# Two hybrid diffusion layers: the gate tiles of the first layer stand at other places in a hand-written order

## The chip, the cores and the metric

The kernel runs on one core of a Trainium2 chip. Its time is the device time of one launch in microseconds; three runs before the change took 2389.72, 2399.01 and 2402.41 us, so the median is 2399.01 us. Times inside a profile are counted from the start of its span.

## The reference, cut to what matters

Two layers work on 512 latent tokens and 256 context tokens of width 1024, in fp32. The part of a layer that this case is about:

```python
proj = a_lat @ w_in[l]             # and proj_c = a_ctx @ w_in[l] in the first layer
q, k, v  = proj[..., Q0:K0], proj[..., K0:V0], proj[..., V0:P0]
p = pool_branch(proj[..., P0:H0], ...)
y = hyena_branch(proj[..., H0:G0], ...)
a = diff_attn_branch(attn_o, ...)
g = sigmoid(proj[..., G0:].reshape(b, l, 3, D_MODEL))
merged = g[:, :, 0] * a + g[:, :, 1] * p + g[:, :, 2] * y
h = h + mod * (merged @ w_out)

def hyena_branch(u, ...):          # 3 x 512 channels
    u = short_conv(u, w_short, b_short)          # 3 taps along the tokens
    v, x1, x2 = split(u, 3)
    z = x1 * fft_long_conv(v, kf[:, 0], bias[0])
    y = x2 * fft_long_conv(z, kf[:, 1], bias[1])
    return y @ w_o
```

The gates `g` (3072 columns, 24 tiles of 128) depend on the normalised input alone and are needed only when the branches are merged, after the attention.

## The kernel before, in words

Activations lie with channels on the partitions and the 768 tokens in the free dimension. Every dense product is made by `units`: one tile of 128 output channels loads its weights (512 KB, a DMA on SP, three buffers `wr`), splits them into a high part (`wh`, ScalarE, line 252) and a low part (`wl`, VectorE, line 253), two buffers of each, and multiplies in three passes per 128 input channels, each for 512 latent and 256 context tokens (line 285). The result stands in an accumulator `d` of PSUM; in the first layer there are two of them. The tile's `evict` takes it out.

The first layer's stage of the long convolution runs over four groups of 128 channels, each with a latent and a context sequence. Its order is written out in the string `PROG[0]`, which `stage` reads letter by letter; capitals are the latent sequence, small letters the context:

- `F`, `f`: the filters and their spectra `K` (`filter_steps`: small matmuls, the window `dec`, absolute sums `fa`, transforms `gre` and `gim`, VectorE combinations at line 654); the latent `K` has one buffer
- `S`, `s`: transposes of the inputs (`vt`, `x1t`) and the forward transform `ur` (lines 767 to 769)
- `1`, `q`: the first spectral product on VectorE (`spectral`: lines 791, 794, 795)
- `M`, `m`: the way back to tokens (`zo`, line 863), the product with `x1`, and forward again
- `2`, `w`: the second spectral product
- `Z`, `z`: the last way back (`yo`, line 880) and the product with `x2` (line 881)
- `h`: one of the three row tiles that the next group needs (`v`, `x1`, `x2`). Its eviction `short` is a ScalarE activation (line 895) and four taps on VectorE (line 899)
- `g`: one gate tile. Its eviction `gate` is a sigmoid on ScalarE (line 935) and a store to device memory (line 936)

The letters give the order in which instructions are handed to a planner. It puts each engine's instructions into a fixed queue by its own costs: of those that are ready it takes the one handed in first. So a `g` or `h` runs while the steps ahead of it wait, and the first letters behind a step are those that fill beside it. Splits of weights are moved ahead (`ahead`, lines 252 and 253).

After group 3's `m` the left half of the fast memory is reopened for the attention. The tiles of head 0 follow (`fill`): value (`vtok`, line 1025), key and query (`roped`: a shuffle and products on VectorE, lines 999 to 1016). Then come the last two letters of the string (`w`, `z`), the right half is reopened, and the attention runs head by head, with `pool` tiles (buffers `pu`, line 1145) and the next head's tiles between. The row maxima of a head's scores are lines 1056 and 1059.

Of the kernel before, what the change touches and what calls it, by code (L numbers as in the profile page):

```python
# [36 lines left out]
NCOL = 129  # L37
FFN_PARTS = ((6, 5, 5, 6), (8, 7, 7))

PROG = ('FggS1ggMfs2gggZgqmFwhhhSz1gMfs2ggZqmFwhhhSz1ggMfs2ggggZggqmFwhhhSz1gMfs2gggZgqm wz',  # L40
        'FgS1gggMFhhhS2ggZgg1gMFhhhS2ggZgg1ggMFhhh2ggSZg1ggggM 2gZ')
HEAD = ("01rfrA23fcrVfBrfU", "01rfrfrA23fVcfBrfU")

# [101 lines left out]
def build(ctx: ExitStack, tc: tile.TileContext, io: dict, out: bass.AP, dbg=None):  # L145
# [763 lines left out]
    def layer(l, a, hs, first, prepare):  # L909
# [73 lines left out]

        early, late = PROG[l].split()
        for what in early:
# [540 lines left out]
```

## Time and profile before

| what | us |
|---|---|
| median of three runs | 2399.01 |
| lowest and highest of them | 2389.72, 2402.41 |
| profiled execution, its own time | 2393.87 |
| its span | 2392.1 |
| TensorE matmul busy, in the span | 2325.6 |
| TensorE weight loads busy | 1981.7 |
| VectorE busy | 1722.3 |
| ScalarE busy | 983.6 |

The busy time of an engine counts the time in which at least one of its instructions runs. Matmuls are pipelined, so that one starts before the one ahead of it has ended. An engine's queue runs in its order: an instruction that waits holds up those behind it. The stage of the long convolution lies between 70 and 500 us of the span; attention of the first layer follows.

### The profile page before, as it was taken

How to read it: one execution, taken by the hardware profiler on the slowest of the kernel's cores; microseconds unless marked ns; L12 is line 12 of the kernel's file. 1: busy time of each engine (PE TensorE's matmuls, PEld its weight loads, DVE VectorE, ACT ScalarE, POOL GpSimd, SP SyncE). 2: the span in 40 equal slices, each digit the busy share in tenths (PEclk: the TensorE clock that was granted, in tenths of full speed). 3: DMA queues.
4: the chain of work that ended last, by engine and by line, in shares of the span. 5: the costliest groups of instructions: out<-in, count | busy, mean ns of one | idle time of the engine just before them, and what ended most of it. 6: DMA issues, size and time to landing. Idle time of an engine off the chain costs nothing. (4 is left out here: it accounts for less than half of the span.)

```text
span 2392.1 us, 33306 instructions
## 1 busy us (share of the span) xinstructions
PE 2325.6 (97%) x12834; PEld 1981.7 (83%) x12834; DVE 1722.3 (72%) x3135; ACT 983.6 (41%) x1657; POOL 2.7 (0%) x8
## 2 busy tenths in 40 slices
PE   6999899999999999999999999999999999999998
PEld 3888688888878878888888888888888789888888
DVE  5688877999888785666768726899888778333336
ACT  6433334367762352121133424433377635312223
POOL 0000000000000000000000000000000000000000
PEclk9999899999989999999999999999999999999999
DMA  7222132321137543444725525344311444332324
GB/s 265 71 96 81 44 103 71 124 95 67 45 133 253 185 156 130 130 146 158 232 88 170 167 98 162 125 165 162 119 56 46 168 152 154 113 97 95 96 92 150
DMA packets 117801, 302.47 MB, mean 126 GB/s; under 512 B 13445, under 2 KB 27397, under 8 KB 116618
## 3 DMA queue, kind: packets, MB, share of 16 engines
q1 hardware_dynamic: 117642, 300.34, 37.9%
q8 instruction: 101, 1.65, 0.3%
q14 instruction: 58, 0.48, 0.1%
HBM read 266.74 MB, written 33.55 MB: 126 GB/s over the span
## 5 line engine op out<-in xcount | busy, mean ns | idle before, releaser
L252 ACT CAST wh<-wr 128x1024 fp32r<-128x1024 f32 (+3 forms) x327 | 331.0, 1013 | 933.2 <-PE d L285 756.1
L285 PE MATMUL d<-ah,wh 128*128 128x512 f32 (+1 forms) x2320 | 707.4, 354 | 6.8 <-ACT si L1371 2.8
L285 PE MATMUL d<-al,wh 128*128 128x512 f32 (+1 forms) x2320 | 709.9, 354 | 0.1
L285 PE MATMUL d<-ah,wl 128*128 128x512 f32 (+1 forms) x2320 | 706.6, 353 | 2.1 <-DVE wl L253 2.0
L253 DVE TENSOR_TENSOR wl<-wr,wh 128x1024 fp32r<-128x1024 f32 (+3 forms) x327 | 383.5, 1173 | 163.4 <-ACT wh L252 153.5
L285 PEld LDWEIGHTS d<-ah,wh 128*128 128x128 f32 x2320 | 387.8, 188 | 71.7 <-ACT si L1371 3.2
L285 PEld LDWEIGHTS d<-ah,wl 128*128 128x128 f32 x2320 | 388.8, 188 | 64.1 <-DVE wl L253 3.0
L285 PEld LDWEIGHTS d<-al,wh 128*128 128x128 f32 x2320 | 389.0, 188 | 61.5 <-DVE al L350 0.8
L489 DVE SCALAR_TENSOR_TENSOR junk<-mr,cb 128x512 bf16<-128x512 f32 x256 | 176.4, 689 | 13.4 <-DMA mr<-in_w_mod_rows_dram 8.2
L285 PE MATMUL d<-hh,wh 128*128 128x512 f32 (+1 forms) x584 | 179.1, 341 | 3.4 <-DVE h L1406 3.4
L285 PE MATMUL d<-hh,wl 128*128 128x512 f32 (+1 forms) x584 | 178.9, 341 | 0.0
L285 PE MATMUL d<-hl,wh 128*128 128x512 f32 (+1 forms) x584 | 178.7, 341 | 0.0
L1380 DVE TENSOR_TENSOR si<-d,si 128x512 f32<-128x512 f32 (+2 forms) x48 | 36.9, 768 | 174.3 <-PE d L285 174.3
L285 PE MATMUL d<-xs,wh 128*128 128x512 f32 x576 | 145.0, 358 | 0.8 <-ACT mx L1183 0.6
L1406 DVE SCALAR_TENSOR_TENSOR h<-d,mod,h 128x512 f32<-128x512 f32 (+1 forms) x96 | 58.5, 615 | 83.3 <-PE d L285 83.0
L285 PEld LDWEIGHTS d<-hh,wh 128*128 128x128 f32 x584 | 102.4, 190 | 17.9 <-issue 3.8
L285 PEld LDWEIGHTS d<-hl,wh 128*128 128x128 f32 x584 | 102.2, 190 | 13.6
L285 PEld LDWEIGHTS d<-hh,wl 128*128 128x128 f32 x584 | 102.4, 190 | 13.1
L285 PEld LDWEIGHTS d<-xs,wh 128*128 128x128 f32 x576 | 94.7, 189 | 18.1 <-ACT mx L1183 0.9
L285 PE MATMUL d<-xs,wl 128*128 128x512 f32 (+1 forms) x288 | 87.7, 358 | 0.0
L795 DVE TENSOR_TENSOR Y<-Y,T 128x1024 f32<-128x1024 f32 (+1 forms) x80 | 84.7, 1059 | 0.2
L794 DVE TENSOR_TENSOR T<-U,K 128x1024 f32<-128x1024 f32 (+1 forms) x80 | 83.1, 1059 | 0.0
(294 smaller groups left out, 3207.8 us busy)
## 6 DMA issues: line engine op xcount, KB each, us to landing
wr<-in_w_in_dram SPq DMA_DIRECT2D x104, 512.0 KB, 3.4
wr<-in_w_ffn_in_dram SPq DMA_DIRECT2D x96, 512.0 KB, 3.3
mr<-in_w_mod_rows_dram SPq DMA_DIRECT2D x160, 256.0 KB, 3.6
wr<-in_w_out_dram SPq DMA_DIRECT2D x32, 512.0 KB, 3.3
ksp<-K SPq DMA_DIRECT2D x28, 384.0 KB, 2.8
K<-ksp SPq DMA_DIRECT2D x8, 1344.0 KB, 7.7
wr<-in_w_ffn_out_dram SPq DMA_DIRECT2D x24, 448.0 KB, 3.4
gsp<-gt SPq DMA_DIRECT2D x24, 384.0 KB, 2.5
```

Source lines behind the costliest of these rows:

```text
L252: A.copy(hi, src)
L253: V.tensor_tensor(out=lo, in0=src, in1=hi.bitcast(F32), op=ALU.subtract)
L285: PE.matmul(o, w[:, c0:c0 + P], x[k][xi][:, c:c + nn], start=(k == 0 and pi == 0), stop=(k == K - 1 and pi == 2))
L489: V.scalar_tensor_tensor(out=junk[:], in0=raw[hf], scalar=1.0, in1=cb[v][hf][:, 0:512], op0=ALU.mult, op1=ALU.mult, accum_out=pv[:, v, hf, ...
L794: V.tensor_tensor(out=t[:], in0=ub, in1=kb, op=ALU.mult)
L795: V.tensor_tensor(out=y[:], in0=y[:], in1=t[:], op=ALU.add)
L1380: V.tensor_tensor(out=sg[f][:, cs], in0=o, in1=sg[f][:, cs], op=ALU.mult)
L1406: V.scalar_tensor_tensor(out=hs[d][:, cs], in0=o, scalar=mods[l][:, 40 + d, s:s + 1], in1=hs[d][:, cs], op0=ALU.mult, op1=ALU.add)
```

## The change

Only the string of the first layer changes. In group 0 one of the two gates between `F` and `S` is taken out; in group 1 a second gate is set beside the first product, a third beside the second product and one ahead of `q`; in group 2 the four gates beside the second product become three and the two ahead of `q` become one. The gates per group go from 8, 3, 8, 5 to 7, 6, 6, 5. The order of the gates among themselves, all other letters and the second layer's string stay.

```diff
-PROG = ('FggS1ggMfs2gggZgqmFwhhhSz1gMfs2ggZqmFwhhhSz1ggMfs2ggggZggqmFwhhhSz1gMfs2gggZgqm wz',
+PROG = ('FgS1ggMfs2gggZgqmFwhhhSz1ggMfs2gggZgqmFwhhhSz1ggMfs2gggZgqmFwhhhSz1gMfs2gggZgqm wz',
         'FgS1gggMFhhhS2ggZgg1gMFhhhS2ggZgg1ggMFhhh2ggSZg1ggggM 2gZ')
```

## Rows read from the trace of the kernel before

**Rows 1.** The page's first lines: span, busy time of the engines.

```profile
span 2392.1 us, 33306 instructions
PE 2325.6 (97%) x12834; PEld 1981.7 (83%) x12834; DVE 1722.3 (72%) x3135; ACT 983.6 (41%) x1657; POOL 2.7 (0%) x8
```

**Rows 2.** Waits of TensorE, 50 to 520 us: total us, times, longest.

```profile
PE yo L880 <- DVE Y L795: 5.3, 1, 5.3
PE fc L694 <- DVE fa L691: 4.9, 1, 4.9
PE ur L767 <- DVE K L654: 1.7, 1, 1.7
```

**Rows 3.** Timeline of TensorE: start, length, engine, line, operation, count, idle before.

```profile
256.14 0.76 PE L694 MATMUL fc<-ones,fa 128*128 128x1 f32 x4 [4.86 <-DVE fa L691]
...
269.39 3.75 PE L880 MATMUL yo<-idft,Y 128*128 128x128 f32 x16 [5.29 <-DVE Y L795]
272.80 0.90 PE L285 MATMUL d<-ah,wh 128*128 128x512 f32 x2
```

**Rows 4.** Line 285 by stretch: length, PE and PEld busy (count), clock, DMA.

```profile
72.70:174.30 101.60, 82.07 (x454) 69.47 (x452) 1.00 0.25 85
174.30:275.90 101.60, 63.64 (x344) 53.23 (x344) 0.93 0.22 72
275.90:377.80 101.90, 81.29 (x443) 67.93 (x443) 1.00 0.27 92
377.80:481.10 103.30, 83.42 (x452) 69.51 (x452) 1.00 0.28 91
```

**Rows 5.** Group 1's stretch, all engines: PE, PEld, DVE, ACT, POOL busy; clock.

```profile
174.30:275.90 101.60, 89.72 (x493) 77.12 (x493) 88.22 (x127) 36.92 (x60) 0.00 (x0) 0.93 0.22 72
```

**Rows 6.** Timeline of ScalarE: three evictions (gate, row tile, value tile).

```profile
163.48 0.80 ACT L935 ACTIVATE gt<-d 128x768 f32<-128x768 f32 x1
...
251.97 0.99 ACT L895 ACTIVATE fm<-d,cols 128x768 f32<-128x768 f32 x1
...
472.21 0.85 ACT L1025 COPY vf<-d 128x512 f32<-128x512 f32 x2
```

**Rows 7.** Timeline of VectorE around the second product of group 1.

```profile
241.44 1.79 DVE L899 SCALAR_TENSOR_TENSOR fm<-d,cols,fm 128x511 f32<-128x511 f32 x3
...
268.02 1.22 DVE L795 TENSOR_TENSOR Y<-Y,T 128x1024 f32<-128x1024 f32 x1
...
270.96 0.48 DVE L899 SCALAR_TENSOR_TENSOR fm<-d,cols,fm 128x255 f32<-128x255 f32 x1
...
276.13 0.48 DVE L899 SCALAR_TENSOR_TENSOR fm<-d,cols,fm 128x255 f32<-128x255 f32 x1
```

**Rows 8.** Tile `wl` in the second products of groups 0, 1, 2: PE, PEld, DVE.

```profile
140.20:168.00 27.80, 11.54 (x44) 6.63 (x43) 3.67 (x3) 1.00 0.32 104
243.70:269.30 25.60, 3.03 (x12) 1.67 (x12) 1.23 (x1) 0.81 0.13 41
343.80:371.00 27.20, 10.86 (x42) 6.25 (x41) 2.45 (x2) 1.00 0.20 68
```

**Rows 9.** Timeline of VectorE and TensorE at the stage's end.

```profile
482.06 0.75 DVE L999 STREAM_SHUFFLE rt<-d 128x512 f32<-128x512 f32 x1
...
493.49 0.74 DVE L999 STREAM_SHUFFLE rt<-d 128x512 f32<-128x512 f32 x1
...
500.00 1.13 PE L880 MATMUL yo<-idft,Y 128*128 128x128 f32 x8
...
502.20 0.68 DVE L1059 TENSOR_REDUCE mx<-s 128x1 f32<-128x512 f32 x1
...
504.03 0.08 DVE L1145 MEMSET pu<- 128x8 f32 x2
```

**Rows 10.** Two stretches of the attention, all engines: PE, PEld, DVE, ACT, POOL.

```profile
500.00:520.00 20.00, 17.90 (x98) 14.31 (x99) 19.19 (x53) 14.94 (x35) 0.00 (x0) 1.00 0.30 102
600.00:620.00 20.00, 20.00 (x121) 17.52 (x120) 16.78 (x39) 13.78 (x34) 0.00 (x0) 1.00 0.16 53
```

## The prediction

> **What bounds the kernel now.** I read the page first [rows 1]: TensorE has work in 2325.6 of 2392.1 us, VectorE in 1722.3. TensorE is the bound over the whole, so a TensorE hole that is filled is worth its length, but only if nothing further on opens one of the same size. The profiled execution took 2393.87 us (its span and 1.8 us around it); the median of the three runs shown is 2399.01, 5.1 us higher. I work with differences and put them on the median.
>
> The list of TensorE's waits between 50 and 520 us has three entries over 1.2 us, 5.3 + 4.9 + 1.7 = 11.9 us [rows 2]. Its timeline puts all three in one place, between 251 and 272 us, in front of the filter sums, the second context spectrum and the way back `Z` of channel group 1 [rows 3]. Everywhere else in this stage TensorE is dense.
>
> Next the stage is cut at the start of each group's context way back, which gives four stretches of 101.6, 101.6, 101.9 and 103.3 us. Of line 285 (gates, row tiles) they ran 454, 344, 443 and 452 matmuls [rows 4]. Group 1 therefore falls short of the mean of the other three (450) by 106. A tile has 8 x 3 x 2 = 48 matmuls and costs 81.29 / 443 x 48 = 8.8 us, so the hole is 2.2 tiles, 19.5 us: the waits, and the granted clock, which is 0.93 there against 1.00 (the 16 matmuls of `Z` took 3.75 us; the level in part of it is 1.2 instead of 2.4 GHz).
>
> What the reader should see in the same rows: the stretch with the hole is **no longer** than the others. TensorE was short of 106 matmuls and the group took 101.6 us as before. So the chain of a group (filter, start, product, middle, product, way back) isn't paced by TensorE but by VectorE and its dependences: busy for 88.22 of 101.6 us in group 1 [rows 5]. In the second product itself it is a wall, one operation behind the other. Gates and row tiles are filler beside that chain.
>
> Why did the filler stop at 251 us? The evictions tell it [rows 6]. A gate leaves PSUM by one ScalarE activation (0.80 us). A row tile (`h`) needs an activation and then four taps of VectorE. In group 1 the three gates were used up before the second product, and the two next tiles were `h`: the second was evicted at 251.97. Of their eight taps three ran at 241.44 ahead of the product; the last of the first tile came at 270.96, the last of the second at 276.13, behind the product's last sum at 268.02 [rows 7]. There are two accumulators `d`; both were held, and the third `h` started at 272.80.
>
> **The change part by part.** No instruction is added or removed: 24 gates, their 24 weight loads on SP, splits, sigmoids and stores, at other places in the order.
>
> (1) Group 0, one gate fewer ahead of `S`. The filter's steps come before gates in the order and gates only fill between them, and the third gate had begun before `S` anyway, so nothing moves up to the seventh gate. In the eighth place (evicted at 163.48 [rows 6]) the first `h` stands now. Its taps wait for the second product's end and slip in beside `Q`, as five taps did within 270.96 to 276.61 [rows 7]. The second `h` takes the other accumulator, so the third may wait: cost 0 to 3 us, I take 1, and it comes out of the lead below.
>
> (2) Group 1, three gates more: six instead of three. Up to 251 us sixteen tiles have run in either version (8 g, 3 h, 3 g, 2 h before; 7 g, 3 h, 6 g now). Now both accumulators are free there, and the two `h` that follow can run at 252 to 269 before they block. The hole closes. TensorE comes out of group 1 ahead by 11.9 (the waits alone) to 19.5 us; I take 16, less the 1 of (1), about 1.7 tiles. Against it stand the splits: each tile puts a VectorE split of 1.22 us into the product. The second product took 25.6 us with one split, 27.2 with two, 27.8 with three [rows 8]. Group 1 gets one or two more, so the chain gets 1.6 to 2.2 us later; I take 1.9.
>
> (3) Group 2, two gates fewer: six and three `h` make nine tiles for a stretch that took 443 / 48 = 9.2. TensorE arrives with the lead, so the first `h` of group 3 runs in the second product and the second beside `Q`: the picture of (1), 0 to 2 us. I take 0, since two accumulators cover it.
>
> (4) Group 3 is as before, but TensorE enters it ahead. Its five gates end some 15 us earlier than before, and the value, key and query tiles of attention head 0 follow. Here I see the lead shrink. In the trace the value tile left PSUM at 472.21 [rows 6], the key's first VectorE step ran at 482.06, the query's at 493.49, the row maxima of head 0 began at 502.20 and the pooling tile's buffer was first written at 504.03 [rows 9]. Key and query leave PSUM by some eight VectorE operations each, behind the same product, and hold both accumulators as `h` did. The tiles after them, pooling 0 and value 1, can be computed but the pooling tile can't be evicted before the right half of the memory is reopened, near 504. By 500 TensorE had already done (500 - 493.5) / 8.8 = 0.74 of the pooling tile; only 2 - 0.74 = 1.26 tiles, 11 us, are there to be done early. If the key's accumulator comes free near 484 (taps slip in beside `Q`) both fit; each us later is lost. Between 0 and 6 us, I take 2.
>
> **Sum.** Lead at the end of the stage: the smaller of 15 and 11 = 11 us; less 1.9 (splits) and 2 (held accumulators): 7 us. After 500 VectorE is full for a time (19.19 of 20 us) while TensorE is too; from 600 on TensorE is full and VectorE has 3 us in 20 to spare [rows 10]. Since the query's eviction also moves ahead, VectorE brings a lead of its own, and I let the 7 us through. 2399 - 7 = 2392 us. Bounds: 11 - 2.2 - 6 = 3 to 11.
>
> **Rivals.**
> (B) The lead is kept whole. If the accumulators come free in time and the attention of head 0 starts earlier with its query, 13 to 18 us arrive: 2383. For it: from 272 to 500 TensorE has no wait over 1.2 us [rows 2], so it is short of nothing but time. Against: the held accumulators of (4).
> (C) VectorE is the pace from 60 to 560 us and nothing is won; what group 1 fills is idled away before the attention: -2 to +4, 2399. For it: stretches of one length with 344 or 443 matmuls [rows 4]. Against: attention from 600 on is TensorE's [rows 10], and 1.26 tiles of it can be done before. The Trainium skill, page "Perfetto Trace Analysis", section "Identifying the Most-Contended Engine", has a rule that speaks for this rival: TensorE is to be judged by the busy share of its weight loads, not of its matmuls, and the engine with the highest share is the one to work on. By it VectorE (88.22 us) stands above TensorE (weight loads 77.12 us) in group 1 [rows 5], and moving TensorE's work would gain nothing there; the rows agree for the group's length, and leave open what the filler is worth later.
> (D) Slower: more filler lengthens the chain. `h` tiles now come early in three groups, and their taps (0.60 us each, from the three at 241.44 [rows 7]) slip in beside `Q`, on whose end the next filter waits: with 4 to 8 taps, some 5 us in each of three groups, and 1.9 of splits, the chain ends 17 us later, at 517. Less the 10 us that the two waiting tiles give back: +7, 2406. It decides from the point where the last `yo` comes later than about 511 instead of 500 [rows 9]. Against: in group 1 five taps slipped in and its stretch was no longer than the others [rows 4, 7].
>
> **How the numbers follow.** Main case 0.52 (2392, its own range 2388 to 2396), B 0.20, C 0.15, D 0.13. A measurement of this kernel tells a change from none at about 0.5%, 12 us. Faster by more: nearly all of B and the lower edge of the main case with what attention's order adds, 0.34. Slower by more: the upper part of D, 0.10. Within: 0.56. The range for 8 in 10 takes in B's upper part, C and D's price: 2379 to 2406.
>
> **What would show it.** Group 1 without a TensorE wait over 2 us between 251 and 273, the granted clock 1.00, about 440 matmuls of line 285 instead of 344; six gate sigmoids between group 0's and group 1's ways back. The four stretches still 101 to 104 us long, the second product of group 1 at 27 to 28 us. The value tile of head 0 evicted near 457 instead of 472, and a new TensorE wait between 473 and 500, where key and query hold both accumulators. The row maxima of head 0 start within 4 us of 502. The forecast is wrong if that new wait is missing and head 0 starts 10 us earlier (B), if the wait is as long as the old one (C), or if the last `yo` comes after 511 (D).

## The result and the profile after

The kernel after took 2409.91 us (median of 6 runs, 2405.3 to 2413.4), the kernel before on the same chip 2397.76 (6 runs, 2389.7 to 2404.3): ratio 1.0057, 95% interval [1.0042, 1.0071]. It is slower by some 12 us; forecast were 2392 us, 7 us faster, and the time lies above the range of 2379 to 2406. The profiled execution took 2408.8 us, 14.9 us more than that of before; that of before lay 3.9 us under its median, this one 1.1 us, so some 3 us of the 14.9 are the choice of execution. One execution of a later kernel (e6) took 3282.7 us at a granted clock of 0.65; its time and its profile are not used.

The page's first lines, to be held against [rows 1]:

```profile
span 2407.0 us, 33305 instructions
PE 2332.3 (97%) x12834; PEld 1988.2 (83%) x12834; DVE 1722.4 (72%) x3135; ACT 981.6 (41%) x1657; POOL 2.7 (0%) x8
```

The same 12834 matmuls are busy 6.7 us longer, and the span minus the busy time, TensorE's idle time, went from 66.5 to 74.7 us. These two, 6.7 and 8.2, are the whole 14.9 us. So two questions are left: where TensorE idles now, and where the same matmuls took longer.

Line 285 by stretch, cut at each context way back, as [rows 4]:

```profile
72.70:175.00 102.30, 80.87 (x446) 68.36 (x444) 1.00 0.24 80
175.00:277.80 102.80, 79.29 (x432) 66.51 (x432) 1.00 0.25 84
277.80:382.00 104.20, 80.48 (x432) 67.40 (x432) 0.98 0.25 83
382.00:486.00 104.00, 79.91 (x428) 66.59 (x429) 0.98 0.29 94
```

The hole is closed: group 1 runs 432 matmuls instead of 344, at full clock. But no stretch got shorter, and each is 0.7 to 2.3 us longer than before. TensorE's waits from 50 to 520 us say where the idle time went (total us, times, longest):

```profile
PE zo L863 <- ACT yh L252: 6.6, 3, 2.2
PE d L285 <- DVE k L1016: 5.1, 1, 5.1
PE ur L767 <- ACT zh L252: 1.9, 1, 1.9
PE d L285 <- ACT vf L1025: 1.5, 1, 1.5
...
```

One hole of 11.9 us [rows 2] became three of 2.2 us, one ahead of the context's way back in each of groups 0 to 2, and 8.5 us (1.9 + 1.5 + 5.1) at the end of the stage.

The groups are best compared from the first product of one to that of the next. All engines (PE, PEld, DVE, ACT, POOL busy; clock), first the kernel before:

```profile
111.60:214.70 103.10, 103.10 (x598) 89.22 (x597) 86.90 (x121) 40.91 (x66) 0.00 (x0) 1.00 0.27 89
214.70:316.00 101.30, 89.42 (x494) 76.92 (x493) 83.43 (x118) 35.75 (x60) 0.00 (x0) 0.93 0.19 67
316.00:418.80 102.80, 102.80 (x599) 89.43 (x598) 86.24 (x120) 39.44 (x65) 0.00 (x0) 1.00 0.25 84
```

and the kernel after:

```profile
111.50:215.70 104.20, 101.39 (x588) 87.89 (x587) 87.17 (x121) 40.86 (x67) 0.00 (x0) 1.00 0.24 80
215.70:319.80 104.10, 101.29 (x582) 88.30 (x581) 85.92 (x121) 39.13 (x64) 0.00 (x0) 0.98 0.25 83
319.80:423.80 104.00, 101.48 (x582) 88.47 (x581) 86.20 (x122) 39.15 (x64) 0.00 (x0) 0.98 0.25 83
```

Group 1, with the hole, had been the shortest. It grew by 2.8 us, and VectorE's busy time in it by 2.5 us. Groups 0 and 2 grew by 1.1 and 1.2 us although TensorE runs 10 and 17 matmuls fewer in them. By group 3's first product the chain is 5.0 us late.

How group 0 lost its 1.1 us: VectorE from the context's first product on (start, length, engine, line, operation), in the kernel after:

```profile
169.65 0.74 DVE L899 SCALAR_TENSOR_TENSOR fm<-d,cols,fm 128x511 f32<-128x511 f32 x1
...
172.33 0.48 DVE L899 SCALAR_TENSOR_TENSOR fm<-d,cols,fm 128x255 f32<-128x255 f32 x1
172.72 0.68 DVE L795 TENSOR_TENSOR Y<-Y,T 128x512 f32<-128x512 f32 x1
...
175.02 0.69 DVE L253 TENSOR_TENSOR yl<-Y,yh 128x512 fp32r<-128x512 f32 x1 [0.17 <-ACT yh L252]
```

Two taps of a row tile (1.22 us) stand inside the product. In the kernel before a gate stood in that place and no tap came until the product was split; its last sum there is this one:

```profile
171.93 0.69 DVE L795 TENSOR_TENSOR Y<-Y,T 128x512 f32<-128x512 f32 x1
```

It ends at 172.62, that of the kernel after at 173.40, 0.8 us later. TensorE, whose last filler started at 172.35, then waits for the product:

```profile
175.04 0.39 PE L863 MATMUL zo<-yh,idfth 128*128 128x256 f32 x1 [2.19 <-ACT yh L252]
```

The end of the stage, TensorE:

```profile
475.89 0.61 PE L285 MATMUL d<-ah,wh 128*128 128x512 f32 x2 [1.54 <-ACT vf L1025]
...
489.80 0.51 PE L767 MATMUL ur<-zh,dfth 128*128 128x256 f32 x2 [1.85 <-ACT zh L252]
...
496.54 1.01 PE L285 MATMUL d<-ah,wh 128*128 128x512 f32 x2 [5.09 <-DVE k L1016]
...
506.79 1.05 PE L880 MATMUL yo<-idft,Y 128*128 128x128 f32 x8
```

and what it waited for, on ScalarE and on VectorE:

```profile
453.43 0.83 ACT L935 ACTIVATE gt<-d 128x768 f32<-128x768 f32 x1
474.99 0.85 ACT L1025 COPY vf<-d 128x512 f32<-128x512 f32 x2
```

```profile
496.06 0.43 DVE L1016 TENSOR_TENSOR k<-d,k 64x256 fp32r<-64x256 f32 x1
...
508.45 0.69 DVE L1059 TENSOR_REDUCE mx<-s 128x1 f32<-128x512 f32 x1
```

The last gate leaves PSUM at 453.43, so head 0's tiles are early. They don't get out: the value tile leaves at 474.99 (472.21 before [rows 6]), the key at 496.06, and the tile behind them starts at 496.54. The row maxima start at 508.45 instead of 502.20 [rows 9]: the chain is 6.3 us late. In the next 60 us, the kernel before and then the kernel after:

```profile
500.00:560.00 60.00, 57.87 (x345) 49.50 (x346) 58.38 (x157) 41.16 (x99) 0.00 (x0) 1.00 0.26 88
```

```profile
500.00:560.00 60.00, 54.94 (x319) 47.45 (x319) 54.63 (x147) 35.79 (x86) 0.00 (x0) 0.95 0.27 90
```

TensorE idles 5.1 us here instead of 2.1, and the granted clock is 0.95: for a part of it the level is 1.2 instead of 2.4 GHz, as it is after the waits in the stage (0.98 in two stretches). The rest of the way is cut at the row maxima and at the first activation of the feed-forward part (line 1371), before:

```profile
502.20:888.50 386.30, 373.54 (x2186) 322.76 (x2184) 332.08 (x746) 218.99 (x435) 0.00 (x0) 0.98 0.41 138
888.50:2392.10 1503.60, 1481.43 (x7996) 1266.39 (x7996) 993.92 (x1795) 549.29 (x871) 1.04 (x2) 1.00 0.40 131
```

and after:

```profile
508.45:901.10 392.65, 375.50 (x2188) 324.81 (x2186) 330.12 (x737) 219.24 (x435) 0.00 (x0) 0.97 0.41 135
901.10:2407.00 1505.90, 1484.58 (x7996) 1269.09 (x7996) 993.72 (x1795) 548.29 (x871) 1.04 (x2) 1.00 0.41 131
```

Of the 14.9 us, 6.3 are there at the row maxima, 6.3 more come between them and the feed-forward part (4.4 us of idling, 2.0 of busy time), and 2.3 behind it. There the same 7996 matmuls are busy 3.2 us longer, nearly half of the 6.7 us, and no wait of the stage is shown to be the reason.

### The profile page after: what moved, and what is told of

Its sections match the earlier page's. It is cut to its first block, busy times and chain, and to the rows that moved or that the text cites. A ratio compares the mean times of both kernels' runs of the same rounds, so it can differ in the third digit from the quotient of the medians.

```text
span 2407.0 us, 33305 instructions
## 1 busy us (share of the span) xinstructions
PE 2332.3 (97%) x12834; PEld 1988.2 (83%) x12834; DVE 1722.4 (72%) x3135; ACT 981.6 (41%) x1657; POOL 2.7 (0%) x8
## 5 line engine op out<-in xcount | busy, mean ns | idle before, releaser
L285 PEld LDWEIGHTS d<-ah,wh 128*128 128x128 f32 x2320 | 391.0, 190 | 80.1 <-DVE k L1016 5.3
L489 DVE SCALAR_TENSOR_TENSOR junk<-mr,cb 128x512 bf16<-128x512 f32 x256 | 176.3, 689 | 12.8 <-DMA mr<-in_w_mod_rows_dram 7.5
```

Of the source, the lines that this page charges most:

```text
L285: PE.matmul(o, w[:, c0:c0 + P], x[k][xi][:, c:c + nn], start=(k == 0 and pi == 0), stop=(k == K - 1 and pi == 2))
L489: V.scalar_tensor_tensor(out=junk[:], in0=raw[hf], scalar=1.0, in1=cb[v][hf][:, 0:512], op0=ALU.mult, op1=ALU.mult, accum_out=pv[:, v, hf, ...
```

## The experiments

All times stand against runs of the kernel before on the same chip, medians 2395.2 to 2396.8 us. "Idle" is the stretch minus TensorE's busy time, from 60 to 500 us (the stage) and from 500 to 560 (head 0). "Group 1" is the stretch from its first product to the next group's. The runs stand on several chips, so the ratio is the better measure of two of them. The windows of the idle time are fixed, and the stage does not begin at the same time in all profiles: in those of e5, e8 and e18 some 6 us later than in that of the kernel after.

| kernel | median us | ratio to before [95%] | idle 60-500 | idle 500-560 | group 1 |
|---|---|---|---|---|---|
| before | 2395-2398 | 1 | 12.0 | 2.1 | 101.3 |
| after | 2409.9 | 1.0057 [1.0042, 1.0071] | 17.5 | 5.1 | 104.1 |
| e1 after, early copies | 2403.3 | 1.0026 [1.0014, 1.0037] | 8.2 | 9.6 | 103.9 |
| e2 before, early copies | 2395.3 | 0.9990 [0.9978, 1.0002] | 12.1 | 2.3 | |
| e3 no gates in the stage | 2585.7 | one run | 159.9 | 1.9 | 108.9 |
| e4 gates 8, 5, 6, 5 | 2407.9 | 1.0044 [1.0028, 1.0059] | 16.1 | 5.1 | 105.6 |
| e5 after, yh on VectorE | 2410.1 | 1.0059 [1.0046, 1.0071] | 12.6 | 7.3 | 105.2 |
| e6 e1 and e5 together | 2406.3 | 1.0039 [1.0026, 1.0052] | | | |
| e7 8, 4, 8, 4, early copies | 2403.8 | 1.0038 [1.0026, 1.0050] | 10.1 | 8.8 | 103.8 |
| e8 gates 7, 4, 8, 5 | 2404.8 | 1.0038 [1.0024, 1.0052] | 18.2 | 3.0 | 102.9 |
| e9 before, no taps | 2402.5 | 1.0022 [1.0011, 1.0033] | 12.8 | 4.0 | 105.0 |
| e10 after, no taps | 2399.1 | 1.0014 [1.0003, 1.0025] | 11.6 | 4.0 | 101.3 |
| e11 before, gates not split | 2398.2 | 1.0005 [0.9993, 1.0017] | 9.5 | 3.6 | 100.5 |
| e12 after, gates not split | 2380.2 | 0.9932 [0.9910, 0.9954] | 1.9 | 1.1 | 97.2 |
| e13 after, splits on GpSimd | 2415.2 | 1.0091 [1.0074, 1.0108] | 22.5 | 2.0 | |
| e14 before, splits on GpSimd | 2437.0 | 1.0174 [1.0157, 1.0191] | 35.6 | 2.3 | |
| e15 e13 and early copies | 2418.8 | 1.0107 [1.0089, 1.0125] | 23.1 | 2.3 | |
| e16 after, half the gates split | 2400.3 | 1.0012 [1.0000, 1.0024] | 10.9 | 3.2 | 104.7 |
| e17 after, group 1's not split | 2405.6 | 1.0033 [1.0019, 1.0048] | 15.4 | 5.2 | 101.4 |
| e18 after, rows copied out too | 2408.2 | 1.0042 [1.0026, 1.0058] | 2.6 | 20.6 | 103.9 |

The theories in the order in which they came: first, that what is lost is lost at the end of the stage, in held accumulators; then, that ScalarE's queue makes the groups late; last, that VectorE's work between the steps of a group sets the group's length, against TensorE's filler or the held accumulators. Each set of expectations numbers its own theories.

**The end of the stage (e1, e2).** Head 0's first value, key and query tiles are copied out of the accumulator at once:

```diff
+def staged(acc):
+    t = TH("hd")
+    for o, c0, n in acc.pieces():
+        A.copy(t[:, c0:c0 + n], o)
+    return [(t[:, c0:c0 + n], c0, n) for c0, n in acc.rng]
 # roped, vtok
+    if cx and mt % 4 == 0:
+        segs = staged(acc)
```

> The changed kernel, but the value, key and query tiles of attention head 0 leave their accumulator at once by one ScalarE copy (0.85 us) into a buffer of the free h ring, and all further steps read that. Theory 1 (the filled hole came back at the end of the stage because these tiles held both accumulators): the new TensorE waits near 475 and 496 us (1.5 and 5.1 us) go, pooling tile 0 starts some 8 us or more earlier, and the time falls by 5 to 12 us to 2398 to 2405. Theory 2 (only the later VectorE chain counts, last yo at 506.8 instead of 500.0): the waits go, but attention's row maxima still start at 508 and the time stays at 2407 to 2413.

> The kernel before with the same early copies. It has no lead to keep when it comes to these tiles, so theory 1 expects less than in the changed kernel: 0 to 5 us faster, 2392 to 2398. Theory 2 expects no change, 2395 to 2400.

The kernel after gains 6.6 us by its medians (the intervals of the ratios don't overlap), the kernel before nothing. So about half of the 12 us hung on the held accumulators. The stage of e1:

```profile
60.00:500.00 440.00, 431.79 (x2479) 375.62 (x2478) 357.22 (x503) 175.50 (x282) 1.47 (x2) 0.99 0.25 83
```

In this stretch TensorE runs 30 matmuls more than in the kernel before (2449), where the kernel after runs 30 fewer (2419), and yet e1 is slower than the kernel before: the time that it was ahead comes back as 9.6 us of idling in head 0.

**The gates taken out, and group 0 left alone (e3, e4).** e3 has no `g` in the string, its 24 tiles run in the last head; e4 keeps group 0 as before:

```diff
-'FgS1ggMfs2gggZgqmFwhhhSz1ggMfs2gggZgqmF...'
+'FS1Mfs2ZqmFwhhhSz1Mfs2ZqmFwhhhSz1Mfs2ZqmFwhhhSz1Mfs2Zqm wz'      # e3
+'FggS1ggMfs2gggZgqmFwhhhSz1ggMfs2gggZqmFwhhhSz1ggMfs2gggZgqm...'  # e4
```

> All 24 gates are taken out of the stage's string and run in the last attention head instead; everything is computed. It shows the chain of the four groups without its filler. Chain paced by VectorE and its dependences (both theories): a group's stretch shrinks only by the splits of the gates that leave, 6 x 1.22 = 7 us, to 93 to 98 us, with TensorE idle for more than half of it, and the whole is slower by over 100 us. If TensorE's queue paced the chain, a stretch would shrink to 60 us or less.

> Gates 8, 5, 6, 5: group 0 as in the kernel before, groups 1 to 3 filled as in the changed one up to the gate ahead of q in group 1. TensorE's lead into group 3 is the same as in the changed kernel. Theory 1 and 2: 2406 to 2412, as the changed kernel. If the missing gate of group 0 (row tiles that run beside its second product and way back) were the cost: 2398 to 2403.

In e3 the groups are about as long as with the gates (93 to 98 us was expected):

```profile
110.50:213.00 102.50, 76.61 (x389) 64.79 (x388) 83.06 (x119) 31.88 (x55) 0.00 (x0) 0.82 0.11 37
213.00:321.90 108.90, 66.01 (x298) 53.11 (x296) 87.51 (x139) 34.27 (x59) 0.00 (x0) 0.73 0.16 52
321.90:421.10 99.20, 45.86 (x148) 34.35 (x148) 69.84 (x102) 23.43 (x45) 0.00 (x0) 0.60 0.06 20
```

TensorE idles for a quarter to over a half of each, but this decides less than it seems to: the granted clock fell to 0.60 to 0.82, so the chain's own matmuls took longer, and the row tiles moved up, so that group 2 has none of them. It is a bound only. e4 takes back group 0's gate: its stretch is 103.1 us again, without a wait, but group 1 takes 105.6, and the time is that of the kernel after within the intervals. Group 0's missing gate alone is not the cause.

**ScalarE's queue (e5, e6).** In the kernel after a row tile's activation stands ahead of `yh` in ScalarE's queue:

```profile
276.28 0.98 ACT L895 ACTIVATE fm<-d,cols 128x768 f32<-128x768 f32 x1
277.17 0.60 ACT L252 CAST yh<-Y 128x512 fp32r<-128x512 f32 x1
```

So `yh` was cast on VectorE (e5), and together with the early copies (e6):

```diff
-split_to(yh[:], yl[:], y[:])
+V.tensor_copy(yh[:], y[:])
+V.tensor_tensor(out=yl[:], in0=y[:], in1=yh[:].bitcast(F32), op=ALU.subtract)
```

> The kernel after, with the high part of the spectral product (yh, ahead of both ways back, first layer) cast on VectorE instead of ScalarE; the order of the gates is unchanged. Theory 1 (the stage is paced by the chain of a group, and the row tile's activation that stands ahead of yh in ScalarE's queue lengthens it in three groups): the three waits of zo for yh (6.6 us in all, 2.2 us each) fall below 0.5 us each, the way back m of group 3 starts 3 to 5 us earlier than the kernel after's 486.0, the row maxima 2 to 5 us earlier than 508.45, and the time is 2403 to 2407. Theory 2 (what is lost is lost at the end of the stage and in the attention, whose filler was used up early; the groups' lateness is covered): m earlier by the same, but the row maxima stay within 1 us and the time at 2408 to 2411. Against both: the cast takes VectorE's time ahead of the weight split, and m is not earlier.

> The kernel after with both repairs: head 0's first value, key and query tiles copied out of the accumulators at once by ScalarE, and yh cast on VectorE. Theory 1: the two add up, 6 us of the first and 3 to 6 us of the second, 2397 to 2401, row maxima at 500 to 503. Theory 2: as with the first repair alone, 2402 to 2405.

The waits stay, only their releaser changes:

```profile
PE zo L867 <- DVE yh L859: 7.2, 3, 2.4
```

The time is unchanged, and together with the early copies it is no better than with these alone (2397 to 2405 was expected, 2406.3 came). The gain that theory 1 forecast did not come, but e5 doesn't test it cleanly: the cast now stands behind a weight split in VectorE's queue and starts 1.4 us after the product's end in group 1, where it had started 0.8 us after it on ScalarE. For group 0 the trace of the kernel after says more: the cast starts 1.0 us behind the product's end in either kernel, so the 0.8 us by which `zo` starts later are those of the product on VectorE.

**Other spreads (e7, e8).** Only the string differs (and e1's copies in e7): `g` 8, 4, 8, 4 and 7, 4, 8, 5.

> Gates 8, 4, 8, 4 over the four groups, with the early copies out of the accumulators of head 0's first tiles: groups 0 and 2 as in the kernel before, one more gate in group 1, one fewer in group 3. Theory 1: no row tile's activation stands ahead of yh within 2 us of it in any group, so no wait of zo for yh over 0.5 us; TensorE's hole in group 1 is one tile shorter (5 to 8 us instead of 11.9), which buys nothing because the chain is as long as before: 2393 to 2397, the same as the kernel before. A rival, that TensorE's sum paces the stage after all: 2385 to 2391. Theory 2: 2396 to 2402, as the lead again runs out in the attention.

> Gates 7, 4, 8, 5, nothing else changed against the kernel before: one gate of group 0 given to group 1. Theory 1: one wait of zo for yh of 2 us, in group 0 alone, 1 to 2 us of lateness from there on, row maxima at 503 to 505, time 2396 to 2401. Theory 2: the lead is one tile only and not lost at the end, 2393 to 2397. If a fuller group 1 alone made the kernel slow (chain steps behind the filler's matmuls), the lateness would begin in group 1, by about 1 us per tile, and group 0 would cost nothing.

Both missed: 2393 to 2397 and 2396 to 2401 were expected, 2403.8 and 2404.8 came. Neither spread reaches the kernel before. In e4 and e7 group 0 is as before and the lateness begins in group 1 (105.6, 103.8 us), as the last rival of e8 has it: steps of the chain that stand behind the filler's matmuls. In e8 group 0 costs 1.1 us as well. No run tests this rival by itself. Against the kernel before, e7's idle time falls by 1.9 us in the stage and grows by 6.7 in head 0.

**VectorE's work taken away (e9 to e12).** Once the taps of the row tiles, once the splits of the 24 gate tiles are left out, in both kernels:

```diff
-for tap, (a0, b0) in ((0, (1, 0)), (24, (0, 1))):
+for tap, (a0, b0) in ((0, (1, 0)), (24, (0, 1))) if l else ():    # e9, e10
-split_to(wh[:, 0:n], wl[:, 0:n], raw[:, 0:n])
+A.copy(wh[:, 0:n], raw[:, 0:n]); wl = wh                         # e11, e12, gates only
```

> The kernel before with the four taps of each row tile of the first layer left out (line 899: 2.4 us of VectorE per tile, 7.3 us per group), so its output is another. It is the base for the next run. Theory A (what VectorE does between the steps of a group sets the group's length): groups 0 to 2 are 1 to 5 us shorter each, row maxima at 490 to 499 instead of 502.2, time 2383 to 2394. Theory B (TensorE's own work in its order sets it, VectorE's small items are covered): groups 0 and 2, where TensorE never waited, stay at 101 to 103, row maxima at 499 to 502, time 2393 to 2397.

> The kernel after without the taps, likewise. Theory A: without the taps that slip between the context's product and its way back, the three waits of zo for yh (2.2 us each) fall below 1 us, and the kernel stands only 4 to 7 us above the kernel before without taps (what is lost at the end of the stage). Theory B: the waits of 2.2 us stay, and it stands 10 to 14 us above, as after stands above before with them.

> The kernel before with the weights of the 24 gate tiles of the first layer not split: the second of the three passes' weights is the high part again, so VectorE has 24 x 1.22 = 29 us less to do beside the groups and TensorE exactly as much as before; the output differs. VectorE as what paces the stage (theory A): row maxima 10 to 25 us earlier than 502.2. TensorE as what paces it in the groups where it never waited (theory B): groups 0, 2 and 3 keep 101 to 103 us, the hole in group 1 shrinks by at most the four splits there (5 us), row maxima at 496 to 502.

> The kernel after without the splits of the gates' weights, likewise. Theory A: its groups shorten as much as those of the kernel before, and it stays 8 to 14 us above it. Theory B: group 1, now without a hole, is TensorE's, and the stretches fall by no more than the waits for yh (2.2 us each); it stays 4 to 12 us above, with the waits at the end of the stage unchanged.

e9, e10 and e12 came outside what either theory expected; the row maxima of e11, at 498.2, lie where theory B put them. Without the splits the kernel after gains 30 us and stands below the kernel before, which gains nothing; without the taps it gains 11 us, the kernel before loses 6, and the two are the same within the intervals. For the kernel before this looks like theory B (nothing to be had from VectorE), for the kernel after without splits like theory A, and more than it expected: neither theory had the two kernels differ. The windows of e12 from first product to first product, and of the stage:

```profile
108.00:206.40 98.40, 98.40 (x571) 85.20 (x571) 79.08 (x113) 39.00 (x64) 0.00 (x0) 1.00 0.24 83
206.40:303.60 97.20, 97.20 (x571) 84.97 (x570) 79.06 (x114) 38.09 (x63) 0.00 (x0) 1.00 0.23 79
303.60:401.80 98.20, 98.20 (x574) 85.33 (x572) 79.23 (x115) 37.71 (x64) 0.00 (x0) 1.00 0.25 88
...
60.00:500.00 440.00, 438.12 (x2534) 379.34 (x2532) 352.05 (x541) 185.01 (x309) 1.47 (x2) 1.00 0.26 88
```

Each group is 5.8 to 6.9 us shorter than in the kernel after, with 7 to 8 us less of VectorE; TensorE's work over the whole is the same. The row maxima start at 484.3. But the groups of e11 have as little VectorE work, and are not as short:

```profile
108.20:208.30 100.10, 100.10 (x582) 86.78 (x581) 79.23 (x113) 39.30 (x65) 0.00 (x0) 1.00 0.24 82
208.30:308.80 100.50, 91.28 (x502) 78.79 (x502) 79.00 (x114) 35.67 (x60) 0.00 (x0) 0.92 0.19 67
308.80:413.50 104.70, 104.69 (x611) 91.18 (x610) 79.39 (x115) 40.67 (x67) 0.00 (x0) 1.00 0.27 91
```

In groups 0 and 2 TensorE has no idle time; group 1, which keeps its hole, has 4.4 us less of VectorE than in the kernel before and is 0.8 us shorter. In e9, without taps, the planner fills group 1 of the kernel before as well, and the hole turns up at the end of the stage with the same wait for the key (5.2 us), and a kernel with less work is slower.

**The splits on GpSimd (e13 to e15).** Everything is computed, the gates' low parts by the idle engine:

```diff
-split_to(wh[:, 0:n], wl[:, 0:n], raw[:, 0:n])
+A.copy(wh[:, 0:n], raw[:, 0:n])
+G.tensor_tensor(out=wl[:, 0:n], in0=raw[:, 0:n], in1=wh[:, 0:n].bitcast(F32), op=ALU.subtract)
```

> The kernel after with the low part of the 24 gate tiles' weights (wl, line 253) computed by GpSimd instead of VectorE; everything is computed. If VectorE's 24 x 1.22 = 29 us are what the spread gates cost (theory A), the stretches of groups 1 to 3 fall from 103 to 104 to 97 to 100, as without the splits, and the time to 2380 to 2390. If the gain without the splits came from work left out or from another plan by chance, 2400 to 2412. If GpSimd is slow (over 4 us a split) or takes VectorE's access to memory away, VectorE's products beside it take longer than 1.06 us on the mean and most of the gain is lost: 2395 to 2405.

> The kernel before with the same splits on GpSimd. Theory A: its groups 0, 2 and 3 are TensorE's (it never waited there), so as without the splits nothing is won, 2394 to 2400, and the hole of group 1 stays at 8 to 12 us.

> The kernel after with the splits on GpSimd and with the early copies of head 0's first tiles out of the accumulators. Theory A: the two repairs add up only so far as waits at the end of the stage are left with the splits on GpSimd: 0 to 5 us below the run without the early copies, 2377 to 2388.

All three are slower than any of the forecasts. Much of the reason stands in the rows of e13, GpSimd and VectorE:

```profile
250.94 3.19 POOL L277 TENSOR_TENSOR wl<-wr,wh 128x1024 fp32r<-128x1024 f32 x1 [11.59 <-ACT wh L276]
```

```profile
251.94 2.75 DVE L253 TENSOR_TENSOR gl<-g,gh 128x512 fp32r<-128x512 f32 x1
```

An operation that takes VectorE 0.69 us elsewhere lasts 2.75 us beside the split, and both end within 0.6 us of one another. About half of what VectorE was spared it lost again (344.3 us busy from 60 to 500 us instead of 358.4, where 29 us of splits were taken away), and GpSimd's splits came late for TensorE (5.4 us of waits). The run can't say whether VectorE's time was the cause.

**The dose (e16, e17).** e12's edit for every second gate, and for the six of group 1 alone (`one=range(28, 52, 2)`, `one=range(35, 41)`).

> The kernel after with the weights of every second gate tile of the first layer not split (12 of 24; the high part stands for the low one, so the output differs): 12 x 1.22 = 15 us of VectorE less. If VectorE's time is what the spread gates cost (theory A), about half of the 30 us that all 24 gave: 12 to 18 us below the kernel after, 2392 to 2398, each of the stretches of groups 1 to 3 by 2 to 4 us shorter. If the 30 us were one arrangement that happens to fit, the result is near one of the ends, 2405 to 2411 or 2380 to 2385.

> The kernel after with only the six gate tiles of group 1 not split: 6 x 1.22 = 7.3 us of VectorE less, all of it in the group that the change filled. Theory A: group 1's stretch falls from 102.8 by 2 to 6 us, the others stay, and the time is 4 to 9 us below the kernel after: 2401 to 2406. Otherwise 2408 to 2412.

Groups 0 and 1 of e17:

```profile
113.20:218.60 105.40, 103.21 (x591) 89.50 (x589) 82.38 (x117) 40.89 (x66) 0.00 (x0) 0.98 0.25 82
218.60:320.00 101.40, 99.51 (x579) 86.31 (x578) 84.09 (x119) 39.33 (x64) 0.00 (x0) 1.00 0.24 82
```

Group 1 is back at the length of the kernel before, but this is no clean dose: splits run ahead of their tiles, so four of the six left group 0's stretch, which is 1.2 us longer for 4.8 us less of VectorE, and two left group 1's, which is 2.7 us shorter for 1.8 us less. Both together are 1.5 us shorter for 6.6. The medians fall by 4.3 us with 6 splits, 9.6 with 12, 29.8 with all 24: more splits left out, more gain, but not in proportion, and the 4.3 us are not clear of noise (the intervals of e17 and of the kernel after overlap). e16 fell short of its 12 to 18 us; its groups 1 and 2 took 104.7 and 102.6 us, and the waits for the key (4.1 us) and the value tile stayed. Only in e12 do they go too.

**The accumulators freed everywhere (e18).** e1's copies, and the same for the row tiles, so that VectorE's taps hold no accumulator:

```diff
 # short
+if l == 0 and ahead[0]:
+    t = TH("hd"); ... A.copy(t[:, c0:c0 + nn], o)
+    segs = [(t[:, c0:c0 + nn], c0, nn) for c0, nn in acc.rng]   # activation and taps read t
```

> The kernel after with head 0's first tiles and also the row tiles of groups 1 to 3 copied out of the accumulators by ScalarE at once, so that no tile holds an accumulator until VectorE has read it; VectorE has exactly the work of the kernel after. Held accumulators as the cause: the three waits of 2.2 us go, the groups are 1 to 2 us shorter each, TensorE idles under 10 us between 60 and 560 us, and the time is 2394 to 2399. VectorE's chain as the cause: the stretches stay at 103 to 105 us, the idle time appears again in attention head 0 (10 to 15 us between 502 and 560), and the time is 2400 to 2406, no better than with the first copies alone (2403).

Group 1, the stage and head 0 (this profile's stage begins 5.7 us later than that of the kernel after):

```profile
221.00:324.90 103.90, 103.55 (x602) 89.86 (x602) 85.88 (x120) 41.84 (x67) 0.00 (x0) 1.00 0.25 83
60.00:500.00 440.00, 437.36 (x2534) 379.56 (x2533) 359.05 (x511) 185.75 (x295) 1.47 (x2) 1.00 0.26 85
500.00:560.00 60.00, 39.39 (x209) 33.76 (x210) 57.01 (x155) 33.62 (x80) 0.00 (x0) 0.79 0.27 89
```

```profile
PE yo L880 <- DVE Y L795: 10.2, 1, 10.2
PE sc L1070 <- DVE junk L489: 6.2, 1, 6.2
```

TensorE idles 2.6 us up to 500 us, at full clock, and has run 2534 matmuls, as many as in e12. The groups take 103.8, 103.9 and 105.4 us all the same, and 20.6 us of idling follow at once: 10.2 ahead of the last `yo` and 6.2 in head 0, both waiting for VectorE. The time is that of the kernel after within the intervals, above what either theory expected. So freeing the accumulators does not make the groups short. e12 and e18 both keep TensorE full in the stage; what e12 has less is VectorE's work, and it is 28 us faster. e18 isn't without a cost of its own, though: its copies give ScalarE 15 us more to do in the stage (185.8 us instead of 170.5), and VectorE waits mostly for ScalarE.

**All of them side by side.** Groups 0 to 2, from the first product to that of group 3, in us:

| kernel | length | VectorE busy | TensorE busy |
|---|---|---|---|
| before | 307.2 | 256.6 | 295.3 |
| after | 312.3 | 259.3 | 304.2 |
| e9 before, no taps | 308.8 | 240.7 | 308.2 |
| e10 after, no taps | 308.0 | 240.7 | 307.9 |
| e11 before, gates not split | 305.3 | 237.6 | 296.1 |
| e12 after, gates not split | 293.8 | 237.4 | 293.8 |
| e17 after, group 1's not split | 311.0 | 252.5 | 304.1 |
| e18 after, rows copied out too | 313.1 | 259.6 | 312.8 |

Each against its own base, e9 has 15.9 us less of VectorE and is 1.6 longer, e11 19.0 less and 1.9 shorter, e10 18.6 less and 4.3 shorter, e12 21.9 less and 18.5 shorter. So VectorE's work by itself does not set the length of the groups.

## Why the prediction was wrong

**What bounds the kernel.** Its reading of the lengths was right and its conclusion wrong. It saw that the group with the hole is no longer than the others, and still held that a filled hole is worth its length if nothing further on opens one. e18 fills all of them, and one opens further on that is larger. That it is VectorE which paces the chain, as the prediction says, no run shows: e11 took 19 us of VectorE's work out of three groups, and they are 1.9 us shorter.

**Step (1), group 0**, taken at 1 us: 1.1 us. **Step (2)**, the hole closes: right, 432 matmuls against about 440, and clock 1.00; the second product at 27 to 28 us: right (27.6, from 243.24 to 270.81). The way back comes 1.9 us later (277.8 against 275.9), which is the forecast figure by luck: 0.7 us of it are group 0's. Not in the step is that the rest of the group gets longer as well: 2.8 us from first product to first product. Two more splits (2.4 us) stand in it; that they are the reason is not shown (e17). **Step (3), group 2**, taken at 0: 1.2 us. The chain at the first product of group 3 is so 5.0 us late where 1.9 were counted. VectorE's busy time is 2.7 us of that, its waits the rest.

**Step (4) is the one that failed.** A lead of 11 us was to pass the end of the stage and 2 us of it to be lost to the accumulators that key and query hold. The new wait was named in its place and between 473 and 500 us, but it took all: 8.5 us of waits, the value tile held as well (forecast near 457, came at 474.99). By 500 us TensorE is not ahead but 30 matmuls behind (2419 against 2449 from 60 us on), and the row maxima, forecast within 4 us of 502, start at 508.45. And what the sum adds, that the lead is let through into the attention, is wrong in itself: with the accumulators freed (e1) the lead does arrive, and head 0 idles 9.6 us for it. Nothing in the main case stands for the 6.3 us that the attention then takes longer, nor for the 2.3 behind it.

**The rivals.** C had it in kind, what group 1 fills is idled away before or in the attention (its condition, that VectorE is the pace, is not shown); its price of -2 to +4 left out that the groups get longer. D had the sign; its last `yo` was to come after 511 and came at 506.79, with 5 us of lateness in the groups instead of 17, and the rest from a place that D didn't name. B is excluded: not even a lead kept whole (e18) helps.

On the rule quoted with C, that the engine with the highest busy share, TensorE by its weight loads, is the one to work on (the Trainium skill, "Perfetto Trace Analysis", "Identifying the Most-Contended Engine"): in group 1 of the kernel after it points to TensorE, 88.30 us of weight loads against 85.92 of VectorE. e18 kept TensorE without idle time in the stage and won nothing; e12 took work from VectorE and won 30 us, e11 took as much from it and won nothing. So between two engines so near each other the share doesn't decide here.

**The sum as it came out**, from the medians: 6.6 of the 12 us hang on the end of the stage (e1). The other half no run separates: the groups' 5.0 us of lateness, the clock's lower level behind the waits, and the attention are in it. From the row maxima to the feed-forward part the profile of the kernel before takes 386.3 us and that of e2, with the same string, 386.2; the other kernels with a profile, e3 and e6 aside, take 388 to 394.

**What stays open.** Each run changes VectorE's load and, through the planner, the order of all queues. What sets the groups' length is not shown. That it is VectorE's work rests on e12 alone; e9, e10 and e11 speak against it as the only cause, and e17 doesn't decide. A rival that no run excludes is TensorE's own queue: in e9, e10, e12 and e18 TensorE is busy for nearly the whole length of the groups, so the filler that the order puts between two steps of the chain can set the length too. How much of e12's 30 us is VectorE's time and how much the order that came with it is not separated (half the splits gave a third). The kernel before, relieved by the same 29 us (e11), has its row maxima 4.0 us earlier, at 498.2, and loses this up to the feed-forward part, which it reaches in 391.0 us instead of 386.3; why is open. A version that computes everything and beats the kernel before was not found.

## What to carry to other kernels

Before a hole is filled, look at the length of its stretch: if the stretch is no longer than its neighbours that have no hole, something other than that engine's amount of work sets the length, and filler moved in can come out again as a hole further on. Count for each piece of filler what it asks of the other engines and buffers, its splits, its evictions and the accumulator that it holds. And follow a lead to where it would be used: the place must have work of the chain to start earlier, not only filler to have done. And do not call an engine the pace of a chain before its work was taken away in both kernels: here leaving out the splits helped in one of them alone.

## What the runs showed of the hardware

In e13 GpSimd takes 2.41 us (median of 24, the longest 11.7) for the split that VectorE does in 1.22, and while it does, a VectorE operation with two inputs waits: 2.75 us instead of 0.69, and the products' sums took 1.21 us on the mean instead of 1.07. The Trainium skill says so ("SBUF — State Buffer", section "SBUF: two separate sides"): the port pair that both engines share is locked for a whole instruction, and the other blocks. The rows agree: the operation ends 0.56 us after GpSimd's does. The forecast of e13 had named such a block, with 2395 to 2405 us; 2415.2 came.

With TensorE's tiles taken out (e3) the granted clock fell to 0.60 to 0.82 by stretch where it is 0.98 to 1.00 with them, and the matmuls `gre<-gh,dfth` of the filters took 613 ns on the mean instead of 449: filler that does nothing for the chain keeps the clock up for the chain's own matmuls.
